# Stick-breaking attention in one inference step: two narrow tiles of each head run as one of 64 columns

## The chip, the core and the metric

The kernel runs on one core of a Trainium2 chip. A core has a matrix engine (PE, with its weight loads shown apart as PEld), a vector engine (DVE), an activation engine (ACT), a general engine (POOL) and a queue that issues most transfers (SP). The engines run side by side, each in its own program order, and wait for one another through semaphores. The metric is the device time of one execution in microseconds (us), as the median of several runs; lower is better.

## What is computed

One layer of a hybrid decoder: a combined input projection, stick-breaking attention in 8 heads of 128 beside gated linear attention in 4 heads, gates, and an output projection, for a prompt of 16 learned and 1024 given positions and for 32 sample positions with a paged cache. The change concerns only the prompt's attention:

```python
def stick_break_weights(z, mask):
    sp = jnp.where(mask, jax.nn.softplus(z), 0.0)
    later = lax.cumsum(sp, axis=z.ndim - 1, reverse=True) - sp
    return jnp.where(mask, jnp.exp(jax.nn.log_sigmoid(z) - later), 0.0)

def sb_attend(qb, qpos, k, v, kpos, bias):
    a = stick_break_weights(sb_logits(qb, k, bias), kpos[None, :] < qpos[:, None])
    return jnp.einsum('bhqk,bkhd->bqhd', a.astype(v.dtype), v)
```

A query sees only keys at strictly earlier positions. The weight of a key needs the sum of the softplus values of all later keys, so key tiles are worked from the last to the first, and a tile hands a running sum (the carry) to the one before it.

## The kernel before, in words

**The stage.** Eight heads follow one another. For each head the projections of v, k and q (`inproj`, L331 to L348) run as 24 steps each; a step, called a beat, is six wide matmuls (L342 to L344). Everything else of the stage is woven between the beats: generators are put on a list with `W.spawn`, and `W.beat()` runs those that are due. A `yield n` in a generator means "go on n beats later". The tile framework then fixes one order for each engine; an engine waits at the head of its queue, and nothing behind overtakes.

**The tiles.** A head's 1024 prompt queries are two halves, qi 1 (positions 528 to 1039) and qi 0 (positions 16 to 527). Keys lie in nine tiles of 126 keys (`KT`) in 128 rows; row 0 of a tile carries the running sum and row 127 is empty. `attend` (L631) spawns a tile for each pair (qi, j) in `ORDER` (L641): (1,8) down to (1,0), then (0,4) down to (0,0), with 2 to 5 beats between spawns by width. Because of the causal mask the first tile of each half is a sliver: (1,8) has 32 query columns and (0,4) has 24. Then come 158 and 150 columns, 284 and 276, 410 and 402, and 512.

**A tile** (`attend_tile`, L578): three matmuls make the logits z (L589 to L591; all products here are split into a high and a low part). DVE and ACT form softplus (L595 to L598), POOL clears what the mask excludes (L601). Two beats later ACT copies the carry out of the previous tile's z into row 0 (L607), waiting beat by beat until it is there; `split_tmp` makes the high part on ACT (L574) and the low part on DVE (L575). `D1` = 4 beats later two matmuls with the triangle `ntri0` add the sums to z (L610, L611); ACT takes the exponential (L615), POOL masks again (L617), and it is split again. `D2` = 6 beats later three matmuls with the values V add the tile's part into the output bank O (L623 to L625). O is one bank with one buffer; the first tile of a half takes it, and after tile j = 0 ACT copies it out (L628) and SP stores it (L629).

**Around it.** `head` (L663) makes the k tiles from the projection (`split_k`, L685, eight casts on ACT and eight subtractions on DVE for a head) and has k and v stored (`tok_out`); `load_v` (L554) reads v back by key tile, into V (L566, L568). `sample_q` (L648) copies q and a small product `zns` of the samples out. On DVE, the logits of the samples against the cached pages (`z_feed`, L464, the tile `jk`) are spread over this stage and the next at one page each two beats.

Of the kernel before, what the change touches and what calls it, by code (L numbers as in the profile page):

```python
# [10 lines left out]
F32 = mybir.dt.float32  # L11
# [5 lines left out]
ALU = mybir.AluOpType  # L17
# [3 lines left out]
P = 128  # L21
# [6 lines left out]
NSMP = NB * NT  # L28
T = META + SEQ + NSMP
REAL = META + SEQ  # L30
# [10 lines left out]
KT = 126  # L41
# [43 lines left out]
def hybrid_step(ctx: ExitStack, tc: tile.TileContext, x_prompt, x_sample, cache_k, cache_v, state_gla,  # L85
# [3 lines left out]
    nc = tc.nc  # L89
    mm = nc.tensor.matmul  # L90
    vec, act, pool = nc.vector, nc.scalar, nc.gpsimd
# [17 lines left out]
    W = Weaver()  # L109

    def stage(nm, dt=F32):
        return stg.tile([P, 384], dt, tag="stg", name=nm)
# [39 lines left out]
    znd = dram.tile([NSMP, HEADS, NSMP], F32, name="znd")  # L152
# [37 lines left out]
    with tc.tile_pool(name="xp", bufs=2) as xp, tc.tile_pool(name="xps", bufs=5, space=PSUM) as xps:  # L190
# [336 lines left out]
    with tc.tile_pool(name="sp", bufs=1) as sp, tc.tile_pool(name="sps", bufs=1, space=PSUM) as sps:  # L527
# [26 lines left out]
        def load_v(h, V, behind):  # L554

            for c in range(3):
                st = stage(f"vr{h}_{c}")
                sv = st[:].rearrange("p (a d) -> p a d", d=P)
                nt = 3 if c < 2 else 2
                src = new_v_prompt[0, 0, :, h, :]  # L560
                pool.memset(st[:], 0.0)
                nc.sync.dma_start(sv[1:KT + 1, :nt], src[c * 378:c * 378 + nt * KT].rearrange("(a p) d -> p a d", p=KT))
                if c == 2:
                    nc.sync.dma_start(sv[1:33, 2, :], src[8 * KT:REAL])
                vs = slice(3 * c, 3 * c + 3)
                ins = act.copy(V[0][:, vs, :], sv)  # L566
                tc.add_manual_dep(ins.ins, behind.name, NOSYNC, reason="behind")
                vec.tensor_tensor(V[1][:, vs, :], sv, V[0][:, vs, :].bitcast(F32), ALU.subtract)  # L568
                yield 1

        def split_tmp(X, rows, n, nm):
            a = sp.tile([P, 512], F32R, tag="hi", bufs=3, name=f"hi_{nm}")
            b = sp.tile([P, 512], F32R, tag="lo", bufs=3, name=f"lo_{nm}")
            act.copy(a[:rows, :n], X)  # L574
            vec.tensor_tensor(b[:rows, :n], X, a[:rows, :n].bitcast(F32), ALU.subtract)  # L575
            return a, b

        def attend_tile(h, qi, qlo, qhi, j, jmax, q, kt, V, carry, O):  # L578
            nm = f"{h}_{qi}_{j}"
            k0 = j * KT  # L580
            nk = P
            c0 = max(qlo, k0)
            col = c0 - qlo
            n = qhi - c0
            qs = slice(c0 - META, c0 - META + n)
            ks = slice(j * P, j * P + nk)
            z = sps.tile([P, 512], F32, tag="z", bufs=4, name=f"z{nm}")
            zz = z[:nk, :n]
            mm(zz, kt[0][:, ks], q[0][:, qs], start=True, stop=False)  # L589
            mm(zz, kt[0][:, ks], q[1][:, qs], start=False, stop=False)  # L590
            mm(zz, kt[1][:, ks], q[0][:, qs], start=False, stop=True)  # L591
            bias = bias0[:nk, h:h + 1]
            xt = sp.tile([P, 512], F32, tag="X", bufs=3, name=f"X{nm}")
            X = xt[:nk, :n]
            vec.tensor_scalar(X, zz, bias, 30.0, ALU.add, ALU.min)  # L595
            act.activation(X, X, AF.Exp)
            act.activation(X, X, AF.Ln, bias=1.0)
            vec.scalar_tensor_tensor(X, zz, bias, X, ALU.add, ALU.max)  # L598
            w = min(n, k0 + KT - c0)
            if w > 0:  # L600
                pool.affine_select(X[:, :w], X[:, :w], [[1, w]], ALU.is_gt, 0.0, base=c0 - k0 + 1, channel_multiplier=-1)  # L601
            yield 2
            if j < jmax:
                while carry.get(qi, (None,))[0] != j + 1:
                    yield 1
                _, cz, ccol = carry[qi]
                act.activation(X[0:1, ccol - col:], cz[0:1, :], AF.Copy, scale=-1.0)  # L607
            sh, sl = split_tmp(X, nk, n, "s" + nm)
            yield D1
            mm(zz, ntri0[:nk, :nk], sh[:nk, :n], start=False, stop=False, skip_group_check=True)  # L610
            mm(zz, ntri0[:nk, :nk], sl[:nk, :n], start=False, stop=True, skip_group_check=True)  # L611
            carry[qi] = (j, zz, col)
            yt = sp.tile([P, 512], F32, tag="X", bufs=3, name=f"Y{nm}")
            Y = yt[:nk, :n]
            act.activation(Y, zz, AF.Exp, bias=bias)  # L615
            if w > 0:
                pool.affine_select(Y[:, :w], Y[:, :w], [[1, w]], ALU.is_gt, 0.0, base=c0 - k0 + 1, channel_multiplier=-1)  # L617
            ah, al = split_tmp(Y, nk, n, "a" + nm)
            yield D2
            if j == jmax:  # L620
                O[qi] = sps.tile([P, 512], F32, tag="O", name=f"O{h}_{qi}")
            o = O[qi]
            mm(o[:, col:], V[0][:nk, j, :], ah[:nk, :n], start=(j == jmax), stop=False, skip_group_check=True)  # L623
            mm(o[:, col:], V[0][:nk, j, :], al[:nk, :n], start=False, stop=False, skip_group_check=True)
            mm(o[:, col:], V[1][:nk, j, :], ah[:nk, :n], start=False, stop=(j == 0), skip_group_check=True)  # L625
            if j == 0:
                st = sp.tile([P, 512], F32, tag="X", bufs=3, name=f"ost{h}_{qi}")
                act.copy(st[:], o[:])  # L628
                nc.sync.dma_start(od[h][:, qlo - META:qhi - META], st[:])  # L629

        def attend(h, q, kt, V):  # L631

            carry, O = {}, {}
            for qi, j in ORDER:
                qlo, qhi = ((16, 528), (528, REAL))[qi]
                n = qhi - max(qlo, j * KT)
                W.spawn(attend_tile(h, qi, qlo, qhi, j, (qhi - 1) // KT, q, kt, V, carry, O))
                yield 2 if n < 100 else 3 if n < 200 else 4 if n < 450 else 5

        D1, D2 = 4, 6  # L640
        ORDER = [(1, j) for j in range(8, -1, -1)] + [(0, j) for j in range(4, -1, -1)]  # L641

        def values(h, behind):
            V = [sp.tile([P, 9, P], F32R, tag=f"V{i}", name=f"V{i}_{h}") for i in range(2)]
            W.spawn(load_v(h, V, behind))
            return V

        def sample_q(h, qsm, ks):  # L648

            ps = sps.tile([P, 512], F32, tag="z", bufs=4, name=f"qst{h}")  # L650
            nc.tensor.transpose(ps[:NSMP, 0:P], qsm[:], ident[:])
            qtok = stage(f"qtok{h}")[:NSMP, :P]
            act.copy(qtok, ps[:NSMP, 0:P])
            nc.sync.dma_start(qsd[:, h * P:(h + 1) * P], qtok)
            ps = sps.tile([P, 512], F32, tag="z", bufs=4, name=f"zn{h}")
            mm(ps[:NSMP, :NSMP], ks[:], qsm[:], start=True, stop=True)
            zns = sp.tile([NSMP, NSMP], F32, tag="zns", name=f"zns{h}")
            act.copy(zns[:], ps[:NSMP, :NSMP])
            nc.sync.dma_start(znd[:, h, :], zns[:])
            yield 4  # L660
            heads_ready.append(h)

        def head(h):  # L663
# [15 lines left out]
            kt = [sp.tile([P, KW], F32R, tag=f"k{i}", name=f"k{i}_{h}") for i in range(2)]  # L679
# [3 lines left out]
            ks = sp.tile([P, NSMP], F32, tag="ks", name=f"ks{h}")  # L683

            def split_k(raw, c, lo, hi):  # L685
                at, end = lo, min(hi, REAL)
                while at < end:
                    j, off = divmod(at, KT)
                    n = max(1, (end - at) // KT) if off == 0 else 1
                    w = min(KT - off, end - at)  # L690
                    d = [t[:, j * P:(j + n) * P].rearrange("p (a x) -> p a x", a=n)[:, :, off + 1:off + 1 + w] for t in kt]
                    r = raw[:, at - lo:at - lo + n * w].rearrange("p (a x) -> p a x", a=n)
                    act.copy(d[0], r)
                    vec.tensor_tensor(d[1], r, d[0].bitcast(F32), ALU.subtract)
                    at += n * w
                if c == 2:
                    act.copy(ks[:], raw[:, REAL - lo:hi - lo])
                return
                yield
# [21 lines left out]
            V = values(h, copied[-1])  # L721
# [15 lines left out]
    with tc.tile_pool(name="gp", bufs=1) as gp, tc.tile_pool(name="gps", bufs=1, space=PSUM) as gps:  # L737
# [323 lines left out]
        for g in range(GH):  # L1061
            kt = gp.tile([P, T], F32, tag="k", name=f"gk{g}")
# [227 lines left out]
    with ExitStack() as out:  # L1290
# [347 lines left out]
        kept = []  # L1638
# [53 lines left out]
```

## Time and profile before

| | |
|---|---|
| median of 3 runs | 2067.45 us (2066.13 to 2067.91) |
| the profiled execution | 2066.38 us, its span 2064.6 us |
| matmuls (PE) in the program | 12507, busy 2024.8 us |
| heads, start of tile (1,8) to start of the next head's | 92.0 to 94.3 us |
| the tiles (1,8) and (0,4) | 8 matmuls each in each of 8 heads |

The span starts with the first instruction of the program and ends with the last; 1.8 us of the execution's time lie around it. The attention stage reaches from 116 us to about 860 us. A row of the timeline gives the start and the duration of an instruction or of a run of like ones; the end of a matmul is modelled, so the distance from one start to the next tells more than the duration.

### The profile page before, as it was taken

What the parts mean: (1) busy time and instruction counts of PE and PEld (TensorE: products, weight loads), DVE (VectorE), ACT (ScalarE), POOL (GpSimd) and SP (SyncE); (2) the same over time, 40 slices, a digit from 0 to 9 for tenths busy, and PEclk for the clock granted to TensorE, in tenths of its full rate; (3) what the DMA queues carried; (4) which work ended last, traced back from release to release, by engine and by line L of the source; (5) the groups of instructions that cost most, each with busy time, mean ns of one, the idle gap of its engine ahead of it and who ended that gap; (6) DMA issues with size and microseconds to landing.
All of it is one profiled execution on the core that took longest, in us unless ns stands there. A gap on an engine that the chain in (4) does not pass through costs nothing.

```text
span 2064.6 us, 41985 instructions
## 1 busy us (share of the span) xinstructions
PE 2024.8 (98%) x12507; PEld 1863.6 (90%) x12507; DVE 1552.7 (75%) x6282; ACT 953.4 (46%) x2293; POOL 84.6 (4%) x304
## 2 busy tenths in 40 slices
PE   6999999999999999999999999999999999999998
PEld 5999999999999998999999999998888898788776
DVE  7368989888988989899798897978544347454576
ACT  7355555565655656433534335343433325332332
POOL 0012000101000000000000000000000000000000
PEclk9999999999999999999999999999999999999999
DMA  6354454544455442533433433335776666452485
GB/s 202 103 139 148 139 159 133 171 132 147 146 160 146 140 124 76 139 102 82 108 100 79 125 82 110 98 82 155 236 233 231 220 222 200 139 166 74 129 271 202
DMA packets 371821, 301.85 MB, mean 146 GB/s; under 512 B 42360, under 2 KB 312104, under 8 KB 371592
## 3 DMA queue, kind: packets, MB, share of 16 engines
q1 hardware_dynamic: 371288, 298.64, 48.6%
q8 instruction: 98, 1.61, 0.3%
q14 instruction: 131, 1.07, 0.2%
q10 hardware_dynamic: 304, 0.53, 0.1%
HBM read 241.75 MB, written 57.31 MB: 145 GB/s over the span
## 4 chain that ended last, share of the span: by engine, by line
PE 75%; DVE 12%; DMA 6%; ACT 3%; issue 3%; SPq 0%; POOL 0%; DVEq 0%; ACTq 0%; POOLq 0%
PE acc_g L342 5%; PE acc_g L343 5%; PE acc_g L344 5%; DVE jk L464 5%; PE b L1593 4%; PE b L1595 4%; PE b L1594 4%; PE acc_k L342 3%; PE acc_k L344 3%; PE acc_k L343 3%; PE acc_v L342 2%; PE acc_q L342 2%; PE acc_q L344 2%; PE acc_q L343 2%; PE acc_v L344 2%
## 5 line engine op out<-in xcount | busy, mean ns | idle before, releaser
L464 DVE SCALAR_TENSOR_TENSOR jk<-kp,qb 128x128 f32<-128x128 f32 x2048 | 593.8, 290 | 43.5 <-DMA qb<-qsd 1.7
L342 PE MATMUL acc_g<-hT,wh_g 128*128 128x368 f32 (+2 forms) x768 | 251.4, 327 | 0.5 <-DVE ga L389 0.5
L343 PE MATMUL acc_g<-hT,wh_g 128*128 128x368 f32 (+2 forms) x768 | 247.6, 322 | 0.0
L344 PE MATMUL acc_g<-hT,wl_g 128*128 128x368 f32 (+2 forms) x768 | 247.1, 322 | 0.0
L1593 PE MATMUL b<-ring,f 128*128 128x512 f32 x416 | 164.3, 395 | 3.5 <-ACT gx L521 1.4
L464 DVE DVE_READ_ACCUMULATOR jk<-kp,qb 128x1 f32 x2048 | 167.6, 82 | 0.0
L1594 PE MATMUL b<-ring,f 128*128 128x512 f32 x416 | 162.6, 391 | 0.0
L1595 PE MATMUL b<-ring,f 128*128 128x512 f32 x416 | 162.1, 390 | 0.0
L342 PEld LDWEIGHTS acc_g<-hT,wh_g 128*128 128x128 f32 x768 | 144.5, 188 | 13.3 <-issue 10.8
L343 PEld LDWEIGHTS acc_g<-hT,wh_g 128*128 128x128 f32 x768 | 144.6, 188 | 1.1 <-issue 0.4
L1395 DVE TENSOR_TENSOR ring<-wr,ring 128x512 fp32r<-128x512 f32 x104 | 71.3, 689 | 98.4 <-ACT ring L1394 97.7
L344 PEld LDWEIGHTS acc_g<-hT,wl_g 128*128 128x128 f32 x768 | 144.5, 188 | 0.0
L342 PE MATMUL acc_gv<-hT,wh_gv 128*128 128x400 f32 (+2 forms) x384 | 130.5, 340 | 0.0
L1394 ACT CAST ring<-wr 128x512 fp32r<-128x512 f32 x104 | 64.1, 620 | 139.3 <-PE b L1595 77.0
L342 PE MATMUL acc_k<-hT,wh_k 128*128 128x384 f32 (+1 forms) x384 | 126.4, 329 | 0.0
L343 PE MATMUL acc_gv<-hT,wh_gv 128*128 128x400 f32 (+2 forms) x384 | 125.3, 326 | 0.0
L342 PE MATMUL acc_q<-hT,wh_q 128*128 128x368 f32 (+2 forms) x384 | 125.1, 326 | 0.0
L344 PE MATMUL acc_gv<-hT,wl_gv 128*128 128x400 f32 (+2 forms) x384 | 124.8, 325 | 0.0
L344 PE MATMUL acc_k<-hT,wl_k 128*128 128x384 f32 (+1 forms) x384 | 124.7, 325 | 0.0
L343 PE MATMUL acc_k<-hT,wh_k 128*128 128x384 f32 (+1 forms) x384 | 124.5, 324 | 0.0
L344 PE MATMUL acc_q<-hT,wl_q 128*128 128x368 f32 (+2 forms) x384 | 123.4, 321 | 0.0
L343 PE MATMUL acc_q<-hT,wh_q 128*128 128x368 f32 (+2 forms) x384 | 123.4, 321 | 0.0
(454 smaller groups left out, 5294.3 us busy)
## 6 DMA issues: line engine op xcount, KB each, us to landing
kp<-in_cache_k_dram SPq DMA_DIRECT2D x512, 64.0 KB
vr<-in_cache_v_dram SPq DMA_DIRECT2D x64, 512.0 KB
tf<-in_w_out_dram SPq DMA_DIRECT2D x64, 256.0 KB
td<-tf SPq DMA_DIRECT2D x64, 256.0 KB
qb<-qsd SPq DMA_DIRECT2D x64, 256.0 KB
wr_g<-in_w_in_dram SPq DMA_DIRECT2D x64, 256.0 KB
wr<-td SPq DMA_DIRECT2D x56, 256.0 KB
wr<-in_w_out_dram SPq DMA_DIRECT2D x48, 256.0 KB
```

The costliest lines, as they stand in the source:

```text
L342: mm(acc[c][:, :n], wh, hh[k][:, lo:hi], start=(k == 0), stop=False)
L343: mm(acc[c][:, :n], wh, hl[k][:, lo:hi], start=False, stop=False)
L344: W.mark = mm(acc[c][:, :n], wl, hh[k][:, lo:hi], start=False, stop=(k == NK - 1)).ins
L464: ins = vec.scalar_tensor_tensor(jk[:], kp[:], 1.0, qbs[h, b][:, t, :], ALU.mult, ALU.mult, accum_out=zt[:, t, NPG - 1 - i:NPG - i])
L1394: act.copy(wh, r)
L1395: vec.tensor_tensor(wl, r, wh.bitcast(F32), ALU.subtract)
L1593: mm(bk[:], ah, wh, start=first and k == 0, stop=False, skip_group_check=True)
L1594: mm(bk[:], ah, wl, start=False, stop=False, skip_group_check=True)
L1595: mm(bk[:], al, wh, start=False, stop=last and k == 7, skip_group_check=True)
```

## The change

The two slivers of a head become one tile of 64 columns, run as (1,8). Its columns 0 to 31 are the last 32 queries of half 0 and its columns 32 to 63 the last 32 queries of half 1. In its key tile, rows 1 to 31 hold keys 1008 to 1038 as before, and rows 32 to 55 hold copies of the 24 keys of tile 4 that half 0 needs, put there by two copies on POOL (L727 of the change) and, for V, by one more DMA in `load_v` (L565). The mask is one select over 64 columns and one clearing of 32 rows by 32 columns (`causal`). The query columns are read in two runs of 32 (`queries`).

After the triangle, ACT copies half 0's carry out at once into a small tile `cy` (L630), which takes the buffer of `ks`; half 1's carry is read from z as before. The output of the 64 columns goes to the output bank O, and ACT copies it out into `ob` (L648); then tile (1,7) takes the bank for half 1, and later (0,3) for half 0. When a half is done, DVE adds its 32 columns of `ob` into the staged output (L657), and the store follows. `ORDER` loses (0,4). The copy `zns` of the samples moves from a buffer of its own into the shared staging buffers.

```diff
             if c == 2:
-                nc.sync.dma_start(sv[1:33, 2, :], src[8 * KT:REAL])
+                nc.sync.dma_start(sv[1:32, 2, :], src[8 * KT:REAL - 1])
+                nc.sync.dma_start(sv[32:56, 2, :], src[4 * KT:4 * KT + 24])
...
+            both = j == 8
             c0 = max(qlo, k0)
             col = c0 - qlo
-            n = qhi - c0
+            n = 64 if both else qhi - c0
...
+            def queries(t):
+                if both:
+                    return t[:].rearrange("p (a x) -> p a x", a=2)[:, :, 480:512]
+                return t[:, qs]
+
+            def causal(t):
+                if both:
+                    t = t.rearrange("p (a x) -> p a x", a=2)
+                    pool.affine_select(t, t, [[1 - 24, 2], [1, 32]], ALU.is_gt, 0.0, base=24, channel_multiplier=-1)
+                    pool.memset(t[0:32, 0, :], 0.0)
+                elif w > 0:
+                    pool.affine_select(t[:, :w], t[:, :w], [[1, w]], ALU.is_gt, 0.0, base=c0 - k0 + 1,
+                                       channel_multiplier=-1)
...
-            carry[qi] = (j, zz, col)
+            if both:
+                kept = sp.tile([P, NSMP], F32, tag="ks", name=f"cy{h}")
+                act.copy(kept[0:1, :], z[0:1, 0:32])
+                carry[0], carry[1] = (4, kept, 480), (8, z[:, 32:64], 480)
+            else:
+                carry[qi] = (j, zz, col)
...
+            if both:
+                o = sps.tile([P, 512], F32, tag="O", name=f"Ob{h}")[:, :n]
+                mm(o, V[0][:, j, :], ah[:, :n], start=True, stop=False, skip_group_check=True)
+                mm(o, V[0][:, j, :], al[:, :n], start=False, stop=False, skip_group_check=True)
+                mm(o, V[1][:, j, :], ah[:, :n], start=False, stop=True, skip_group_check=True)
+                O[2] = sp.tile([P, 64], F32, tag="ob", name=f"ob{h}")
+                act.copy(O[2][:], o)
+                return
...
                 act.copy(st[:], o[:])
+                vec.tensor_tensor(st[:, 480:512], st[:, 480:512], O[2][:, 32 * qi:32 * qi + 32], ALU.add)
                 nc.sync.dma_start(od[h][:, qlo - META:qhi - META], st[:])
...
-        ORDER = [(1, j) for j in range(8, -1, -1)] + [(0, j) for j in range(4, -1, -1)]
+        ORDER = [(1, j) for j in range(8, -1, -1)] + [(0, j) for j in range(3, -1, -1)]
...
-            zns = sp.tile([NSMP, NSMP], F32, tag="zns", name=f"zns{h}")
-            act.copy(zns[:], ps[:NSMP, :NSMP])
+            zns = stage(f"zns{h}")[:NSMP, :NSMP]
+            act.copy(zns, ps[:NSMP, :NSMP])
...
                 if c == 2:
+                    for t in kt:
+                        pool.tensor_copy(t[:, 8 * P + 32:8 * P + 56], t[:, 4 * P + 1:4 * P + 25].bitcast(F32))
                     act.copy(ks[:], raw[:, REAL - lo:hi - lo])
```

The orders below are those of the built programs, without times. A row gives the source line (of its own program, so L610 before is L626 in the change), the operation, the tile written and the tiles read, and the shape.

The first place is PE in the first head, at the end of half 1 and the start of half 0; `z_0_4` is the logit bank of tile (0,4), `O_0` the output bank of half 0. Before:

```order
L589 MATMUL z_0_4_2278<-q_0_1072,k_0_842 128x24
L590 MATMUL z_0_4_2278<-q_0_1073,k_0_842 128x24
L591 MATMUL z_0_4_2278<-q_0_1072,k_0_843 128x24
...
L610 MATMUL z_0_4_2278<-hi_s_0_4_2332,ntri_825 128x24
L611 MATMUL z_0_4_2278<-lo_s_0_4_2333,ntri_825 128x24
...
L623 MATMUL O_0_2617<-hi_a_0_4_2444,V_0_1306 128x24
L624 MATMUL O_0_2617<-lo_a_0_4_2445,V_0_1306 128x24
L625 MATMUL O_0_2617<-hi_a_0_4_2444,V_0_1307 128x24
```

In the change the same places hold the next tile, (0,3):

```order
L605 MATMUL z_0_3_2288<-q_0_1074,k_0_842 128x150
L606 MATMUL z_0_3_2288<-q_0_1075,k_0_842 128x150
L607 MATMUL z_0_3_2288<-q_0_1074,k_0_843 128x150
...
L626 MATMUL z_0_3_2288<-hi_s_0_3_2343,ntri_825 128x150
L627 MATMUL z_0_3_2288<-lo_s_0_3_2344,ntri_825 128x150
...
L651 MATMUL O_0_2631<-hi_a_0_3_2445,V_0_1308 128x150
L652 MATMUL O_0_2631<-lo_a_0_3_2446,V_0_1308 128x150
L653 MATMUL O_0_2631<-hi_a_0_3_2445,V_0_1309 128x150
```

The eight matmuls of (0,4) are gone, and all of half 0 moves up by one tile; the projection's matmuls around them stand as before.

The second place is PE in the first head where the 64 columns leave the output bank and tile (1,7) takes it. In the change:

```order
L644 MATMUL Ob_1643<-hi_a_1_8_1443,V_0_1308 128x64
L645 MATMUL Ob_1643<-lo_a_1_8_1444,V_0_1308 128x64
L646 MATMUL Ob_1643<-hi_a_1_8_1443,V_0_1309 128x64
L342 MATMUL acc_v_2_1312<-hT_153,wh_v_2_1600 128x304
...
L651 MATMUL O_1_1739<-hi_a_1_7_1588,V_0_1308 128x158
L652 MATMUL O_1_1739<-lo_a_1_7_1589,V_0_1308 128x158
L653 MATMUL O_1_1739<-hi_a_1_7_1588,V_0_1309 128x158
```

Both wrote one bank `O_1` before, without a copy between; now ACT's copy of `Ob` stands between them. There are 29 other matmuls between L646 and L651.

The third place is ACT in the second head at the time when half 0 ends and the k tiles of the third head are cast (`k_2`; `st_k` are k's stores, `wh_q` the projection's weights). Before, the run of casts stands ahead of the exponential of (0,2) and the split of (0,1):

```order
L574 CAST hi_s_0_2_4335<-X_0_2_4180 128x276
L543 COPY st_k_0_4371<-tk_k_0_4370 128x384
L543 COPY st_k_1_4389<-tk_k_1_4388 128x384
L693 CAST k_2_3660<-kraw_0_4192 128x6
...
L693 CAST k_2_3660<-kraw_2_4259 128x32
L596 ACTIVATE X_0_0_4418<-X_0_0_4418 128x512
...
L615 ACTIVATE Y_0_2_4442<-z_0_2_4176,bias_827 128x276
L607 ACTIVATE X_0_1_4311<-z_0_2_4176 1x276
L574 CAST hi_a_0_2_4445<-Y_0_2_4442 128x276
L574 CAST hi_s_0_1_4451<-X_0_1_4311 128x402
```

In the change it stands behind them, ahead of the exponential of (0,1) and the split of (0,0):

```order
L575 CAST hi_s_0_1_4325<-X_0_1_4245 128x402
L722 CAST k_2_3656<-kraw_0_4179 128x3x126
...
L722 CAST k_2_3656<-kraw_2_4257 128x32
L543 COPY st_k_0_4371<-tk_k_0_4370 128x384
L612 ACTIVATE X_0_0_4358<-X_0_0_4358 128x512
...
L636 ACTIVATE Y_0_1_4432<-z_0_1_4241,bias_827 128x402
L623 ACTIVATE X_0_0_4358<-z_0_1_4241 1x402
L575 CAST hi_a_0_1_4435<-Y_0_1_4432 128x402
L575 CAST hi_s_0_0_4441<-X_0_0_4358 128x512
```

The same run of casts now meets the next tile of half 0, which is wider.

More of the change, by code (lines that the diff above doesn't have):

```diff
@@ L576, in split_tmp, with attend_tile @@
             return a, b
-        def attend_tile(h, qi, qlo, qhi, j, jmax, q, kt, V, carry, O):
+        def attend_tile(h, qi, qlo, qhi, j, q, kt, V, carry, O):
             nm = f"{h}_{qi}_{j}"
@@ L581, in attend_tile @@
             nk = P
+            both = j == 8
             c0 = max(qlo, k0)
             col = c0 - qlo
-            n = qhi - c0
+            n = 64 if both else qhi - c0
             qs = slice(c0 - META, c0 - META + n)
             ks = slice(j * P, j * P + nk)
+            def queries(t):
[10 more added lines that the diff above has]
+                                       channel_multiplier=-1)
             z = sps.tile([P, 512], F32, tag="z", bufs=4, name=f"z{nm}")
             zz = z[:nk, :n]
-            mm(zz, kt[0][:, ks], q[0][:, qs], start=True, stop=False)
-            mm(zz, kt[0][:, ks], q[1][:, qs], start=False, stop=False)
-            mm(zz, kt[1][:, ks], q[0][:, qs], start=False, stop=True)
+            mm(zz, kt[0][:, ks], queries(q[0]), start=True, stop=False)
+            mm(zz, kt[0][:, ks], queries(q[1]), start=False, stop=False)
+            mm(zz, kt[1][:, ks], queries(q[0]), start=False, stop=True)
             bias = bias0[:nk, h:h + 1]
@@ L599, in attend_tile @@
             w = min(n, k0 + KT - c0)
-            if w > 0:
-                pool.affine_select(X[:, :w], X[:, :w], [[1, w]], ALU.is_gt, 0.0, base=c0 - k0 + 1, channel_multiplier=-1)
+            causal(X)
             yield 2
-            if j < jmax:
+            jmax = (3, 7)[qi]
+            if not both:
                 while carry.get(qi, (None,))[0] != j + 1:
@@ L615, in attend_tile @@
             act.activation(Y, zz, AF.Exp, bias=bias)
-            if w > 0:
-                pool.affine_select(Y[:, :w], Y[:, :w], [[1, w]], ALU.is_gt, 0.0, base=c0 - k0 + 1, channel_multiplier=-1)
+            causal(Y)
             ah, al = split_tmp(Y, nk, n, "a" + nm)
@@ L636, in attend @@
                 n = qhi - max(qlo, j * KT)
-                W.spawn(attend_tile(h, qi, qlo, qhi, j, (qhi - 1) // KT, q, kt, V, carry, O))
+                W.spawn(attend_tile(h, qi, qlo, qhi, j, q, kt, V, carry, O))
                 yield 2 if n < 100 else 3 if n < 200 else 4 if n < 450 else 5
         D1, D2 = 4, 6
-        ORDER = [(1, j) for j in range(8, -1, -1)] + [(0, j) for j in range(4, -1, -1)]
+        ORDER = [(1, j) for j in range(8, -1, -1)] + [(0, j) for j in range(3, -1, -1)]
         def values(h, behind):
@@ L656, in sample_q @@
             mm(ps[:NSMP, :NSMP], ks[:], qsm[:], start=True, stop=True)
-            zns = sp.tile([NSMP, NSMP], F32, tag="zns", name=f"zns{h}")
-            act.copy(zns[:], ps[:NSMP, :NSMP])
-            nc.sync.dma_start(znd[:, h, :], zns[:])
+            zns = stage(f"zns{h}")[:NSMP, :NSMP]
+            act.copy(zns, ps[:NSMP, :NSMP])
+            nc.sync.dma_start(znd[:, h, :], zns)
             yield 4
```

## The prediction

> **What bounds the kernel now.** I read the page first: the busy times of the engines, then the chain of work that ended last, followed back from the last instruction, with its shares by engine.
>
> ```profile
> PE 2024.8 (98%) x12507; PEld 1863.6 (90%) x12507; DVE 1552.7 (75%) x6282; ACT 953.4 (46%) x2293; POOL 84.6 (4%) x304
> ...
> PE 75%; DVE 12%; DMA 6%; ACT 3%; issue 3%; SPq 0%; POOL 0%; DVEq 0%; ACTq 0%; POOLq 0%
> ```
>
> PE is busy for 98% of the span, but that is an average over several stages. The change touches only the attention stage, so I asked for the busy times by window: start:end, length, then busy time and count for PE, PEld, DVE, ACT and POOL, and at the end the granted clock.
>
> ```profile
> 116.00:393.00 277.00, 275.19 (x1685) 265.19 (x1684) 244.84 (x1104) 157.29 (x381) 32.34 (x106) 1.00 0.51 144
> ...
> 485.00:578.00 93.00, 91.91 (x562) 88.14 (x561) 82.45 (x378) 52.59 (x127) 7.84 (x27) 1.00 0.50 150
> ...
> 762.00:862.00 100.00, 99.34 (x609) 91.04 (x608) 90.32 (x418) 58.79 (x139) 8.40 (x35) 1.00 0.36 97
> ```
>
> PE is busy for 99% in each of them (275.19 of 277.00) at the full clock. DVE stands close behind: 244.84 of 277.00 is 88%, 90.32 of 100.00 is 90%. ACT has 43% of its time free (1 - 157.29/277.00), POOL far more. So a microsecond taken from PE here counts, as long as DVE, ACT and the carries still deliver in time. The waits of PE's weight loads in the whole stage (waiting line, releaser, total, times, longest) say how well they deliver now:
>
> ```profile
> PEld z L611 <- DVE lo_s L575: 6.2, 13, 1.1
> PEld z L610 <- ACT hi_s L574: 3.3, 5, 1.2
> PEld zn L656 <- issue: 2.2, 8, 0.3
> ```
>
> All eight heads together lose 6.2 + 3.3 = 9.5 us at the triangle matmuls. That is little against 750 us, but it says who is late when someone is: the split of the carried X, on ACT and DVE.
>
> **What the change removes.** The eight matmuls of tile (0,4) go in each of eight heads, 64 in all. A narrow matmul's duration in the timeline overlaps its neighbours', so I price it by starts. First the logits, with the projection's wide matmuls around them:
>
> ```profile
> 167.33 0.17 PE L589 MATMUL z<-q,k 128*128 128x24 f32 x1
> 167.36 0.26 PE L590 MATMUL z<-q,k 128*128 128x24 f32 x1
> 167.47 0.26 PE L591 MATMUL z<-q,k 128*128 128x24 f32 x1
> 167.58 0.42 PE L342 MATMUL acc_k<-hT,wh_k 128*128 128x384 f32 x1
> 167.84 0.34 PE L343 MATMUL acc_k<-hT,wh_k 128*128 128x384 f32 x1
> 168.02 0.33 PE L344 MATMUL acc_k<-hT,wl_k 128*128 128x384 f32 x1
> ```
>
> A wide matmul undisturbed takes 0.17 to 0.18 (167.84 to 168.02). From 167.33 to 167.84 stand three narrow ones and one wide one, 0.51; less 0.17 leaves 0.34 for three. It is not the 24 columns that cost: the first follows its neighbour almost free (0.03 to the next start), and the wide one behind starts its successor late (0.26 instead of 0.17). The triangle pair and the output triple, first start and second wide start behind:
>
> ```profile
> 175.35 0.17 PE L610 MATMUL z<-hi_s,ntri 128*128 128x24 f32 x1
> ...
> 175.75 0.33 PE L343 MATMUL acc_k<-hT,wh_k 128*128 128x384 f32 x1
> ...
> 831.63 0.17 PE L623 MATMUL O<-hi_a,V 128*128 128x24 f32 x1
> ...
> 832.13 0.33 PE L343 MATMUL acc_g<-hT,wh_g 128*128 128x368 f32 x1
> ```
>
> The pair: 0.40 - 0.17 = 0.23. The triple, here of the last head: 0.50 - 0.17 = 0.33. Together 0.34 + 0.23 + 0.33 = 0.90 us a tile, 0.112 us a matmul, and **8 x 0.90 = 7.2 us** for the stage.
>
> The Trainium skill has two rules that bear on this price, and they disagree. In "TensorE: Matmul & The Clock Gate", the section "Back-to-back issue gap" puts a matmul of up to 64 columns at an issue floor of about 25 ns, from which I estimate 64 x 0.025 = 1.6 us for the whole change. The section "LDWEIGHTS (loading the stationary operand)" of that page has a load take its columns over 1.2 in ns, so 107 ns for 128 columns, an estimate of 6.8 us. The trace's 0.112 us sides with the second.
>
> **What becomes wider.** The other sliver grows from 32 to 64 columns. A pair of 158 columns bounds it from above:
>
> ```profile
> 128.26 0.24 PE L610 MATMUL z<-hi_s,ntri 128*128 128x158 f32 x1
> ...
> 128.66 0.34 PE L343 MATMUL acc_v<-hT,wh_v 128*128 128x384 f32 x1
> ```
>
> 0.40 from start to start, as with 24 columns. So between 24 and 158 columns width costs PE nothing, and I take 0 for 64 (bounds 0 and 0).
>
> **What is added off PE.** These rows price it (busy, mean ns):
>
> ```profile
> L595 DVE TENSOR_SCALAR X<-z,bias 128x24 f32<-128x24 f32 x8 | 1.9, 239 | 0.0
> L575 DVE TENSOR_TENSOR lo_a<-Y,hi_a 128x32 fp32r<-128x32 f32 x8 | 1.7, 212 | 0.2
> L607 ACT ACTIVATE X<-z 1x32 f32<-1x32 f32 x8 | 1.4, 174 | 0.0
> L697 ACT COPY ks<-kraw 128x32 f32<-128x32 f32 x7 | 1.5, 218 | 0.2
> L628 ACT COPY ost<-O 128x512 f32<-128x512 f32 x16 | 9.4, 586 | 16.0 <-PE O L625 15.8 <-DVE lo_a L575 0.2
> L601 POOL TENSOR_SCALAR_AFFINE_SELECT X<-X 128x32 f32<-128x32 f32 x8 | 2.2, 280 | 117.5 <-DVE X L598 117.5
> ```
>
> - DVE: two additions of 128x32 a head, 2 x 0.21 = 0.42, against the four operations of (0,4), at up to 0.24 each, that go. DVE gets no fuller, but a head gets shorter by 0.90 too, so its share of 88 to 90% stays. The store now waits behind the addition; its buffer is one of the ring of three that X and Y use, and a head has two takings fewer from that ring than before. I take 0.
> - ACT: the carry copy, about 0.17, and the copy out of the bank, between 0.22 and 0.59 by the rows of 32 and 512 columns (near 0.22 at 64). The exponential, logarithm, casts and carry of (0,4) go, each about as long as the copies. The carry copy stands ahead of Y's exponential, and behind it waits the split of (1,7), some 0.2 us late; cover below.
> - POOL: two key copies of 24 columns, the rest widened, each nearest to 0.28; POOL is free for over 85% of the stage. The key copies wait for DVE's low parts of k, and the masks of X for (0,0) and of (0,1)'s Y stand queued behind them. This is a new wait on POOL, and the last rival is about it.
> - SP: one more transfer of 24 rows for V, behind other loads of V in the third and the seventh head. The `zns` copy takes a shared buffer; without cover it would lengthen the 2.2 us for all heads at `zn` above, which bounds it on the small side. I take 0 for both and price the transfer in a rival.
>
> The new wait I feared most is the output bank: (1,7) cannot take it before ACT has copied 64 columns out.
>
> ```profile
> 225.06 0.43 ACT L574 CAST hi_s<-X 128x284 fp32r<-128x284 f32 x1
> 225.07 0.26 PE L625 MATMUL O<-hi_a,V 128*128 128x32 f32 x1
> ...
> 229.96 0.23 PE L623 MATMUL O<-hi_a,V 128*128 128x158 f32 x1
> ```
>
> The sliver's output ends at 225.33; ACT is then in a cast until 225.49, and even a copy of 0.59 ends at 226.1. The bank is wanted at 229.96. Cover: 3.9 us. Were it gone, each head would stall for what is missing, with the projection's next beats queued behind L651 on PE.
>
> **The sum.** Profiled execution 2066.38 - 7.2 = 2059.2. The median of the runs stands 1.07 above that execution, so I forecast 2059.2 + 1.1 = **2060.3**. Its own range is 2058 to 2062.5: prices of 0.03 us a group (three groups, eight heads, 0.7 us) and the spread of the runs, with a little more upwards for the costs taken at 0.
>
> **The rivals.**
>
> *The stalls shrink too (chance 0.13).* Half 0's tiles start two beats earlier, and its chain of carries has one link of four beats less. The head's end, where the splits are late, gets more air. The second head's 1.66 us (shown below) stand at such a place, (0,1). If 4 of the 9.5 us go, somewhat under half, the time is 2060.3 - 4 = 2056.3. Against it: the waits name ACT and DVE, whose queues stay as full.
>
> *DVE and the transfers keep part (0.13).* In two of the windows the chain leaves PE for long stretches; these are its shares by line in 485:578 and 762:862, then one piece of it in the first, and rows of ACT and PE behind it:
>
> ```profile
> by line: DVE jk L464 11.1%; issue 8.4%; DMA qb<-qsd 6.4%; PE acc_k L342 6.0%; PE acc_k L344 6.0%; PE acc_k L343 6.0%; DMA vr<-out_dram 4.5%; PE acc_q L342 4.1%; PE acc_q L344 4.1%; PE acc_q L343 4.1%; DMA kp<-in_cache_k_dram 3.7%; DVE X L59
> ...
> by line: DVE jk L464 17.5%; issue 10.5%; PE acc_g L342 8.3%; PE acc_g L343 8.0%; PE acc_g L344 8.0%; DMA qb<-qsd 5.1%; DVE X L595 4.8%; DVE lo_s L575 4.6%; ACT X L596 2.8%; ACT X L597 2.8%; DVE wl_g L185 2.5%; ACT Y L615 2.1%; DVE X L598 2.
> ...
> 488.49 4.18 DMA vr<-out_dram
> 492.70 0.51 ACT L566 CAST V<-vr 128x384 fp32r<-128x384 f32 x1 [1.75 <-DMA vr<-out_dram]
> ...
> 505.63 0.40 PE L611 MATMUL z<-lo_s,ntri 128*128 128x284 f32 x1 [0.24 <-DVE lo_s L575]
> ...
> 510.57 0.45 PE L610 MATMUL z<-hi_s,ntri 128*128 128x410 f32 x1 [0.26 <-ACT hi_s L574]
> ```
>
> ACT waits 1.75 for V, and PE waits 0.24 and 0.26 a dozen microseconds later. If the added transfer does this to every head, 8 x 0.5 = 4.0 us go; if only half the heads, 2. With the two heads whose chain runs over DVE's `jk` giving nothing (2 x 0.9 = 1.8), it keeps about 4 of the 7.2: 2064.3. Against it: this wait, in the fifth head, is the only such one that I found, and DVE loses work in every head too.
>
> *The price is the first matmul's, not the group's (0.05).* By the step from 167.33 to 167.36 a narrow matmul costs 0.03 where its load hides behind a wide one. If the other five of a tile found such places too, 64 x 0.03 = 1.9, and 2065.5. Against it: the late wide matmul in all three groups. That the change removed fewer matmuls than it says would give the same; the order of the built program has them gone.
>
> *ACT's run of k casts makes the widest tile late, slower (0.05).* The casts for the next head stood ahead of the split of (0,1), and now stand ahead of that of (0,0), with POOL's key copies waiting for DVE in the same place. In the second head the run is now (ACT, then PE's loads for (0,1)):
>
> ```profile
> 187.10 0.60 ACT L693 CAST k<-kraw 128x114 fp32r<-128x114 f32 x3
> ...
> 191.29 0.42 ACT L574 CAST hi_a<-Y 128x276 fp32r<-128x276 f32 x1 [1.46 <-POOL Y L617]
> 191.62 0.52 ACT L574 CAST hi_s<-X 128x402 fp32r<-128x402 f32 x1
> ...
> 192.19 0.19 PEld L610 LDWEIGHTS z<-hi_s,ntri 128*128 128x128 f32 x1 [1.23 <-ACT hi_s L574]
> 192.81 0.19 PEld L611 LDWEIGHTS z<-lo_s,ntri 128*128 128x128 f32 x1 [0.43 <-DVE lo_s L575]
> ```
>
> Here a mask late on POOL made ACT wait 1.46 and the loads 1.23 + 0.43 = 1.66. If every head came to lose that, 8 x 1.66 = 13.3, and the time would be 2060.3 + 13.3 = 2073.6. It decides from 0.9 us a head (the gain gone) and is measurably slower from 1.4. Against it: 9.5 us over eight heads is 1.2 a head already counted in the time of before, and ACT has 43% of its time free to catch up.
>
> **How the numbers follow.** The forecast has 0.64, the rivals 0.13, 0.13, 0.05 and 0.05. A measurement of this kernel can tell about 0.2%, 4.1 us, from no change: faster means below 2063.3, slower above 2071.6. Faster: 0.64 + 0.13 = 0.77. Within: 0.13 + 0.05 = 0.18. Slower: 0.05. The range takes in the forecast, the shrunk stalls and the kept part, 0.90 of the chance less their outer tails: 2055.5 to 2065.
>
> **What would show it.** The profile should list 64 matmuls fewer, and from (1,8) to the next (1,8) a head about 0.9 us less than the 92.0 to 94.3 of before. Right about the cover: no load of L651 waiting for ACT's `ob`, no wait on `cy`. The first rival shows as fewer than 9.5 us of waits for hi_s and lo_s; the second as ACT waiting for `vr` in more heads; the last as waits at the triangle of (0,0), of 0.9 us or more a head. Wrong altogether would be a head that is shorter by 0.2 us with no new waits: then a narrow matmul is not worth 0.112.

## The result, and the profile after

| | before | after |
|---|---|---|
| median of 13 runs each | 2066.13 us (2062.32 to 2067.91) | 2071.12 us (2069.39 to 2073.27) |
| profiled execution, span | 2064.6 us | 2069.0 us |
| matmuls | 12507 | 12443 |

The change makes the kernel slower: ratio 1.0026, 95% interval 1.0018 to 1.0033. The 64 matmuls are gone, and the time went up by 5 us where 7.2 us less was forecast. The page of the changed kernel, busy times and then the chain's shares by engine:

```profile
PE 2023.6 (98%) x12443; PEld 1859.6 (90%) x12443; DVE 1550.6 (75%) x6266; ACT 947.9 (46%) x2269; POOL 89.1 (4%) x320
...
PE 72%; DVE 12%; DMA 7%; issue 4%; ACT 3%; SPq 1%; POOL 1%; DVEq 0%; POOLq 0%; ACTq 0%
```

The shares of busy time hardly move. PE's share of the chain falls from 75% to 72%, but that share is no measure of the time: two of the variants below, both faster than this kernel, have 72% (e7) and 66% (e8). What tells is the waits of PE's weight loads in the attention stage (waiting line, releaser, total, times, longest); L626 and L627 are the triangle's matmuls in the changed kernel:

```profile
PEld z L627 <- DVE lo_s L576: 8.9, 20, 0.9
PEld z L626 <- ACT hi_s L575: 8.0, 9, 2.5
PEld acc_v L342 <- ACT qsm L749: 2.4, 2, 2.1
```

The waits for the splits grew from 9.5 to 16.9 us, and a wait for `qsm` from 0.2 to 2.4. That is 7.4 + 2.2 = 9.6 us. By the timeline three places stand out.

**The end of the first head, (0,0).** The rows of POOL, ACT and PE, in this order:

```profile
190.82 0.88 POOL L401 TENSOR_SCALAR_AFFINE_SELECT lv<-lv 128x64 f32<-128x64 f32 x2
...
192.01 0.83 POOL L403 TENSOR_SCALAR_AFFINE_SELECT lv<-lv 128x64 f32<-128x64 f32 x2
192.81 0.29 POOL L601 TENSOR_SCALAR_AFFINE_SELECT Y<-Y 128x126 f32<-128x126 f32 x1
...
193.12 0.53 ACT L575 CAST hi_a<-Y 128x402 fp32r<-128x402 f32 x1 [2.00 <-POOL Y L601]
193.56 0.61 ACT L575 CAST hi_s<-X 128x512 fp32r<-128x512 f32 x1
...
194.22 0.49 PE L626 MATMUL z<-hi_s,ntri 128*128 128x512 f32 x1 [2.25 <-ACT hi_s L575]
195.26 0.79 PE L627 MATMUL z<-lo_s,ntri 128*128 128x512 f32 x1 [0.54 <-DVE lo_s L576]
...
196.17 0.52 PE L343 MATMUL acc_q<-hT,wh_q 128*128 128x384 f32 x1
196.49 0.52 PE L344 MATMUL acc_q<-hT,wl_q 128*128 128x384 f32 x1
```

POOL builds level masks (`lv`, from `level_masks`, for a later stage) ahead of the mask of (0,1). ACT waits 2.00 us for that mask with the split of (0,0) behind it, and PE stands for 2.25 and 0.54. Before, the same `lv` work delayed the narrower (0,1), and PE stood for 0.93 and 0.17 (the prediction's rows give the longer waits of its loads). And the price does not end with the stall: the wide matmuls behind it follow one another at 0.32 instead of 0.17. The busy times by window (PE, PEld, DVE, ACT, POOL, then the granted clock) show why:

```profile
194.00:196.00 2.00, 1.24 (x3) 0.83 (x4) 1.93 (x9) 0.17 (x1) 0.00 (x0) 0.76 0.07 15
196.00:198.00 2.00, 2.00 (x8) 2.00 (x7) 1.38 (x11) 1.30 (x2) 1.08 (x3) 0.50 0.58 197
198.00:200.00 2.00, 2.00 (x13) 2.00 (x13) 1.21 (x4) 0.62 (x1) 1.10 (x2) 0.89 0.60 94
```

The granted clock is at half for some 3 us. That loses 1.5 us: from the start of L627 to the next output matmul (L651) it takes 3.66 us here, and 2.20 in e3 below, where the same rows ran at full clock. With it the account closes: 9.6 + 1.5 = 11.1. The attention stage says the same. The first matmul of `acc_gk`, a projection of the next stage, starts 4.0 us later than before, where 7.2 earlier was forecast, so 11.2 are missing (before, then after):

```profile
870.52 0.34 PE L342 MATMUL acc_gk<-hT,wh_gk 128*128 128x400 f32 x1
```

```profile
874.53 0.34 PE L342 MATMUL acc_gk<-hT,wh_gk 128*128 128x400 f32 x1
```

Over the whole span it is 2069.0 - (2064.6 - 7.2) = 11.6 us.

**The triangle of (1,5), 410 columns.** ACT in the first head before (two rows), then ACT and PE after:

```profile
137.75 0.54 ACT L574 CAST hi_s<-X 128x410 fp32r<-128x410 f32 x1
138.19 0.62 ACT L182 CAST wh_k<-wr_k 128x512 fp32r<-128x512 f32 x1
```

```profile
137.82 0.60 ACT L182 CAST wh_k<-wr_k 128x512 fp32r<-128x512 f32 x1
138.33 0.53 ACT L575 CAST hi_s<-X 128x410 fp32r<-128x410 f32 x1
...
138.91 0.46 PE L626 MATMUL z<-hi_s,ntri 128*128 128x410 f32 x1 [0.85 <-ACT hi_s L575]
139.81 0.45 PE L627 MATMUL z<-lo_s,ntri 128*128 128x410 f32 x1 [0.44 <-DVE lo_s L576]
```

Two rows changed places: the cast of the next projection's weights now goes first, and the split that PE waits for is later by its length.

**The start of the third head.**

```profile
308.15 0.51 ACT L567 CAST V<-vr 128x384 fp32r<-128x384 f32 x1 [2.00 <-DMA vr<-out_dram]
308.57 0.19 ACT L749 ACTIVATE qsm<-acc_q 128x32 f32<-128x32 f32 x1
...
308.81 0.41 PE L342 MATMUL acc_v<-hT,wh_v 128*128 128x304 f32 x1 [1.95 <-ACT qsm L749]
```

A cast of V waits for its load with `qsm` queued behind it, and `qsm` holds a bank that PE's next projection needs. Before, `qsm` stood one row ahead of that cast.

### The profile page after: what moved, and what is told of

It reads as the page before. It is cut to its first block, busy times and chain, and to the rows that moved or that the text cites. A ratio compares the mean times of both kernels' runs of the same rounds, so it can differ in the third digit from the quotient of the medians.

```text
span 2069.0 us, 41791 instructions
## 1 busy us (share of the span) xinstructions
PE 2023.6 (98%) x12443; PEld 1859.6 (90%) x12443; DVE 1550.6 (75%) x6266; ACT 947.9 (46%) x2269; POOL 89.1 (4%) x320
## 4 chain that ended last, share of the span: by engine, by line
PE 72%; DVE 12%; DMA 7%; issue 4%; ACT 3%; SPq 1%; POOL 1%; DVEq 0%; POOLq 0%; ACTq 0%
PE acc_g L342 5%; PE acc_g L343 5%; PE acc_g L344 5%; DVE jk L464 5%; PE b L1624 4%; PE b L1626 4%; PE b L1625 4%; PE acc_k L342 3%; PE acc_k L343 3%; PE acc_k L344 3%; PE acc_v L342 2%; PE acc_v L343 2%; PE acc_v L344 2%; PE acc_gq L343 1%; PE acc_gq L342 1%
```

## The experiments

All were timed in five rounds against the kernel before; the ratios have 95% intervals. The theories first went by what was added: **A**, the addition on DVE; **B**, V's added transfer; **C**, POOL's key copies.

**e1, e2: the addition on DVE left out, and moved to POOL.** The reason for A was a new wait in the trace of the change, DVE's total for the addition:

```profile
DVE ost L657 <- ACT ost L656: 8.8, 6, 2.0
```

```diff
-                vec.tensor_tensor(st[:, 480:512], st[:, 480:512], O[2][:, 32 * qi:32 * qi + 32], ALU.add)
+                pool.tensor_tensor(st[:, 480:512], st[:, 480:512], O[2][:, 32 * qi:32 * qi + 32], ALU.add)
```

(e1 has only the first line of it.)

> The changed kernel without the two DVE additions of a head, so the output of the 64 columns is left out of the result; the order of all other work on PE, ACT and POOL stays but for a few rows. Theory A (the addition stands early in DVE's queue, waits there for ACT's copy of the output bank, 8.8 us in six waits, and DVE at 90% busy can't catch up, so the first tiles of the next head are late): the time falls by 4 to 8 us from 2071 to 2063 to 2067, and the waits of PE's loads for hi_s and lo_s fall from 16.9 us to about 10. Theory B (V is late through the added transfer) and theory C (POOL's key copies make masks late): no change, 2070 to 2072.

> The changed kernel with the two additions of a head on POOL instead of DVE; same result. Theory A: like e1, 2063 to 2067, unless POOL's masks queue behind the waiting addition, when some of it comes back. Theories B and C: no change, 2070 to 2072.

Measured: e1 2071.34 us, ratio 1.0025 (1.0015 to 1.0036); e2 2073.97, 1.0034 (1.0021 to 1.0046). A falls. In e1 DVE no longer waits there, and PE's waits are nearly the same:

```profile
PEld z L627 <- DVE lo_s L576: 8.1, 18, 0.8
PEld z L626 <- ACT hi_s L575: 7.8, 8, 2.4
```

DVE's 8.8 us of standing cost nothing that can be measured. On POOL (e2) the addition makes the kernel no faster either.

**e3: without the transfer of 24 rows of V.**

```diff
-                    nc.sync.dma_start(sv[32:56, 2, :], src[4 * KT:4 * KT + 24])
```

> The changed kernel without the added transfer of 24 rows of V, so the values of those 24 keys are left out. Theory B: ACT's waits for vr fall from 9.2 us to about 2 and the time by 2 to 4 us, to 2067 to 2069. Theories A and C: within 1 us of 2071, and ACT's waits for vr stay above 6 us, since V is late because SP's queue waits for DVE.

Measured 2071.32, ratio 1.0025 (1.0015 to 1.0035). B falls: the time stays. In its trace PE's wait for `qsm` is down to 0.6 us, but the waits for the splits are 18.1. ACT still waits for V nearly as long, in the trace of the change and in that of e3:

```profile
ACT V L567 <- DMA vr<-out_dram: 9.2, 6, 3.0
```

```profile
ACT V L566 <- DMA vr<-out_dram: 7.7, 6, 3.0
```

**e4: without POOL's key copies.**

```diff
-                    for t in kt:
-                        pool.tensor_copy(t[:, 8 * P + 32:8 * P + 56], t[:, 4 * P + 1:4 * P + 25].bitcast(F32))
```

> The changed kernel without POOL's two key copies of a head, so the logits of those 24 keys are left out (their key columns stay zero); all other orders stay as they are. Theory C: POOL's 19.1 us of waits for DVE's low parts of k go, masks come earlier, and the time falls by 2 to 4 us, to 2067 to 2069; the stall of 2.25 us at (0,0) of the second head goes. Theories A and B: within 1 us of 2071.

Measured 2073.17, ratio 1.0038 (1.0025 to 1.0051). C falls; PE still stood for 2.26 us at (0,0) of the first head (the expectation calls it the second). No addition taken alone is the cause. The next theories went by what was moved: **S**, the missing tile puts the queues in another order; **N**, the matmuls are worth 7.2 us and the additions together eat them; **P**, they are worth little; **Z**, the buffer that `zns` takes; **L**, the level masks.

**e5: the removal alone, in the kernel before.**

```diff
-        ORDER = [(1, j) for j in range(8, -1, -1)] + [(0, j) for j in range(4, -1, -1)]
+        ORDER = [(1, j) for j in range(8, -1, -1)] + [(0, j) for j in range(3, -1, -1)]
...
-                W.spawn(attend_tile(h, qi, qlo, qhi, j, (qhi - 1) // KT, q, kt, V, carry, O))
+                W.spawn(attend_tile(h, qi, qlo, qhi, j, 8 if qi else 3, q, kt, V, carry, O))
```

> The kernel before with tile (0,4) left out and nothing put in its place (24 columns of half 0 lose 24 keys and their carry), so 64 matmuls fewer and none of the additions. Theory S (the missing tile moves half 0 two beats ahead, the queues of ACT, DVE and POOL are put in another order, and the new order makes the splits late): 2066 to 2071, with longer waits for hi_s and lo_s than the 9.5 us of before. Theory N (narrow matmuls are worth 7.2 us, and what was added eats it): 2058 to 2061. Theory P (a narrow matmul is worth only 0.03 us): 2064 to 2066 with waits as before.

Measured 2067.92, ratio 1.0008 (0.9999 to 1.0017). Taking 64 matmuls out, and putting nothing in, gains nothing over the whole program. The waits of PE's loads (L610, L611 are the triangle here):

```profile
PEld z L611 <- DVE lo_s L575: 6.0, 13, 0.9
PEld z L610 <- ACT hi_s L574: 5.7, 7, 2.5
...
PEld acc_v L342 <- ACT qsm L718: 2.0, 2, 1.0
```

The stall of the first head's end is here too (its row stands in the last section), and the late `qsm`, and ACT waits for V:

```profile
ACT V L566 <- DMA vr<-out_dram: 7.7, 6, 3.8
```

So these come with the removal, not with the additions. Of the 7.2 us, the waits take 4.0 (11.7 + 2.0 against 9.5 + 0.2), and by the trace the stage does end 3.0 us earlier than before. S stands, but behind the stage the trace loses 4.2 us again. Of these, 0.9 is a wait for `gx` (ACT) and 1.5 a half clock at 1444 us, which e6's trace has too and the one of before has not; the rest stays open.

**e6: `zns` alone moved into the staging buffers, in the kernel before.**

```diff
-            zns = sp.tile([NSMP, NSMP], F32, tag="zns", name=f"zns{h}")
-            act.copy(zns[:], ps[:NSMP, :NSMP])
+            zns = stage(f"zns{h}")[:NSMP, :NSMP]
+            act.copy(zns, ps[:NSMP, :NSMP])
```

> The kernel before with zns alone moved into the shared staging buffers; no row of any queue moves. Theory Z (the buffer that zns takes makes the loads of V late, which ACT then waits for): ACT's waits for vr rise from 1.8 us toward 9 and the time by 2 to 4 us, to 2068 to 2070. Theories S and N: within 1 us of 2066.

Measured 2066.32, ratio 0.9999 (0.9990 to 1.0009). Z falls; this part costs nothing, as forecast.

**e7: the change with half 0 held back by two beats.**

```diff
                 yield 2 if n < 100 else 3 if n < 200 else 4 if n < 450 else 5
+                if (qi, j) == (1, 0):
+                    yield 2
```

> The changed kernel with half 0 held back by the two beats that (0,4) took, so that its tiles stand at the beats of before. Theory S: the k casts stand ahead of the split of (0,1) again, the waits fall toward 9.5 us, and the time to 2060 to 2065. Theories N and Z: within 1.5 us of 2071.

Measured 2064.24, ratio 0.9988 (0.9979 to 0.9997): 6.9 us less than the change, and a little faster than before. Two beats of standing back win what was lost. ACT at the end of the first head, before, after, and in e7:

```profile
202.13 0.62 ACT L182 CAST wh_v<-wr_v 128x512 fp32r<-128x512 f32 x1 [2.36 <-PE acc_q L343]
205.00 0.59 ACT L628 COPY ost<-O 128x512 f32<-128x512 f32 x1 [2.25 <-PE O L625]
```

```profile
204.23 0.59 ACT L656 COPY ost<-O 128x512 f32<-128x512 f32 x1 [4.63 <-PE O L653]
205.96 0.62 ACT L182 CAST wh_v<-wr_v 128x512 fp32r<-128x512 f32 x1 [1.14 <-PE acc_q L343]
```

```profile
200.47 0.62 ACT L182 CAST wh_v<-wr_v 128x512 fp32r<-128x512 f32 x1 [4.45 <-PE acc_q L343]
201.31 0.59 ACT L656 COPY ost<-O 128x512 f32<-128x512 f32 x1 [0.22 <-PE O L653]
```

In the change the copy of the output bank stands ahead of the weight cast and holds it back; in e7 the old order is there again. That this swap costs time is not shown: in the change, no matmul of PE waits for another engine from there until 236 us. What e7 wins is seen at the triangle, where the waits fall from 16.9 to 6.3 us. The waits for `qsm` do not fall (4.0 us), so they come with the missing tile, not with the two beats. The third and the seventh head give the price of a sliver: in neither trace does a matmul stand for another engine there (only PE's loads wait, once, 0.4 us before and 0.19 in e7). From the third head's start to the fourth's, before and in e7:

```profile
303.21 0.18 PE L589 MATMUL z<-q,k 128*128 128x32 f32 x1
...
395.24 0.18 PE L589 MATMUL z<-q,k 128*128 128x32 f32 x1
```

```profile
301.55 0.19 PE L605 MATMUL z<-q,k 128*128 128x64 f32 x1
...
392.52 0.19 PE L605 MATMUL z<-q,k 128*128 128x64 f32 x1
```

92.03 became 90.97, 1.06 us less; in the seventh it is 1.03.

**e8: the change with one level mask in each head, at its middle.**

```diff
-            yield 16
+            yield 72
...
-        W.spawn(level_masks(), 30, lasting=True)
+        W.spawn(level_masks(), 20, lasting=True)
```

> The changed kernel with POOL's level masks (lv) built one in each head, at the middle of the head, instead of one each 16 beats; the orders of PE and ACT stay as they are. Theory L (in the second head's preparation, at the end of the first head, the mask of (0,1) stands behind lv on POOL, the triangle of (0,0) stalls for 3.2 us, and PE then runs at half the granted clock for 2 us): the stall at (0,0) of the first head falls from 3.2 us to under 1, the clock stays at 1.00 behind it, and the time falls by 3 to 5 us, to 2066 to 2068. Other theories: within 1 us of 2071.

Measured 2068.15, ratio 1.0010 (1.0001 to 1.0019): 3.0 us less than the change. The mask of (0,1) now delays ACT by 0.38, and PE's triangle of (0,0) has only this left:

```profile
190.98 0.53 ACT L575 CAST hi_a<-Y 128x402 fp32r<-128x402 f32 x1 [0.38 <-POOL Y L601]
...
192.81 0.50 PE L627 MATMUL z<-lo_s,ntri 128*128 128x512 f32 x1 [0.22 <-DVE lo_s L576]
```

L stands, at the low end of what was expected: 2.8 us of stall and the half clock behind it. ACT's run of k casts is where it was, so that run is not what made this tile late.

**e9, e10, e11: the mends together, and the kernel before with two of them.** e9 is e7 with e8; e10 adds one edit, by which V's casts stand behind `qsm`:

```diff
-                    act.activation(qsm[:], ps[:, n:], AF.Copy, scale=QSCALE)
+                    copied.append(act.activation(qsm[:], ps[:, n:], AF.Copy, scale=QSCALE).ins)
```

> The changed kernel with both edits: half 0 held back by two beats (e7) and the level masks in the middle of the heads (e8). Theory S with L as two costs that add: 2064.2 - 3.0, so 2060.5 to 2062.5. If holding half 0 back already took the masks out of the way (L inside S): 2063 to 2065, as e7.

> As e9, and V's casts of a head stand behind the copy of qsm on ACT, which PE's next projection waits for. Theory Q (the 4.0 us of PE's waits for qsm in e7 come from V's late load at the head of ACT's queue): these waits fall under 1 us and the time by 2 to 4 us against e9, to 2058 to 2060. If V's load itself is what PE needs next: the waits move to another line and the time stays within 1 us of e9.

> The kernel before with the level masks in the middle of the heads and qsm ahead of V's casts, as a measure of what the two edits give without the change. Theory S: 1 to 2 us (the stall of 1.55 us at the end of the first head goes), 2064 to 2065.5; if the edits do as much here as behind the change, 2060 to 2062, and the change itself is worth nothing.

Measured: e9 2061.90, ratio 0.9982 (0.9973 to 0.9992); e10 2059.75, 0.9968 (0.9956 to 0.9980); e11 2064.93, 0.9992 (0.9983 to 1.0001). The times fell as expected, but that S and L are two costs that add is not shown. In e7's trace the first head's triangle of (0,0) has no stall left that e8's edit could take. The splits wait 6.3 us in e7 and 6.2 in e9. What differs is the sixth head's start, where PE waits 2.21 us for `qsm` in e7 and 1.03 in e9, and a half clock behind the longer wait (shown below). The intervals of e7 and e9 overlap. In e10 the waits for `qsm` are gone. The kernel before gets little from two of the edits: 1.2 us, not clear of noise.

**e12: the removal alone (e5), half 0 held at its old beats.**

> The kernel before with tile (0,4) left out as in e5 and half 0 held at its beats of before. Theory S with a price of 0.112 us for each of the 64 matmuls: 2059 to 2061. If removal alone is worth less, 2064 to 2066, and the price of a narrow matmul was wrong too.

Measured 2054.41, ratio 0.9940 (0.9927 to 0.9954), a larger gain than the theory expected. What is left of the waits:

```profile
PEld acc_v L342 <- ACT qsm L720: 1.7, 2, 1.3
PEld z L611 <- DVE lo_s L575: 1.6, 4, 0.6
...
PEld z L610 <- ACT hi_s L574: 0.2, 1, 0.2
```

The 9.5 us of before fell to 1.8, so the first rival, in which the stalls shrink too, is what removal does when half 0 keeps its beats: 7.2 + 7.7 - 1.5 (the longer wait for `qsm`) = 13.4, against 11.7 measured, and 12.2 at the end of the stage. Why the waits shrink below those of before is not shown. And e7, the same with the additions, is 9.8 us slower: the additions do cost, although taking one alone out of the shifted order gained nothing.

**e13, e14: the weight cast behind the split of (1,5).** In the built order of the change ACT casts the next k weights ahead of the split of (1,5) in five of the first seven heads. Before it was one of seven, and in e5 and e12 one too, so the additions do this. Four of them do not decide it alone: by the traces it is still five of seven with the addition on DVE, the transfer of V or the key copies left out (e1, e3, e4), and one of seven with `zns` alone moved (e6). The edit ties the cast (the second weight chunk after the split in the program) behind it:

```diff
-            act.copy(a[:rows, :n], X)
+            split_tmp.ins = act.copy(a[:rows, :n], X).ins
...
             sh, sl = split_tmp(X, nk, n, "s" + nm)
+            if (qi, j) == (1, 5):
+                hold.extend([split_tmp.ins, None])
...
-                tc.add_manual_dep(ins, hold.pop().name, NOSYNC, reason="behind")
+                first_in = hold.pop()
+                if first_in is not None:
+                    tc.add_manual_dep(ins, first_in.name, NOSYNC, reason="behind")
```

> The changed kernel with one order put back: ACT's cast of the next k weights (L182) stands behind the split of (1,5), 410 columns, in every head, as it did in six of the first seven heads before; PE's order is untouched. Theory W (the added work lets the scheduler put the weight cast, 0.6 us, ahead of the split in five of the first seven heads, and the triangle of (1,5) waits for it and for DVE's part): the 5.8 us of stalls at 410 columns fall under 2.5 and the time by 2 to 4 us, to 2067 to 2069. If the splits there are late for another reason: within 1 us of 2071.

> As e10, with the order of e13 as well. Theory W: the 4.1 us of stalls at 410 columns left in e10 fall to about 1, and the time from 2059.8 to 2056 to 2058, near the 2054.4 of e12. If not W: within 1 us of 2059.8.

Measured: e13 2069.53, ratio 1.0017 (1.0008 to 1.0026), 1.6 us less than the change, short of the 2 to 4 that were expected and with an interval that overlaps the change's. e14 2056.90, ratio 0.9955 (0.9942 to 0.9969), 2.9 us less than e10. In both the order is as meant, and PE's standing at the triangle of 410 columns falls by 1.4 us, from 3.7 to 2.3 in e13 and from 2.8 to 1.4 in e14, not to the small rest that theory W expected (its 5.8 and 4.1 us are waits of the loads). So the swap is a part of what makes these splits late; the rest stays open. e14 is the fastest version with the whole result of the change: 14.2 us below the change and 9.3 below the kernel before in its own comparison (8.0 below e11, the kernel before with two of the same edits). The waits of e14 (L630, L631 are its triangle):

```profile
PEld z L631 <- DVE lo_s L578: 3.4, 8, 0.7
...
PEld z L630 <- ACT hi_s L577: 1.3, 2, 0.9
```

## Why the prediction was wrong, point by point

- **The bound and the removal: not contradicted.** PE's matmuls went as counted. A head without such stalls became 1.03 to 1.06 us shorter in e7, up to 0.2 of it by shorter waits of the loads; the forecast was 0.90. The price of 0.03 falls: with the beats kept, removal gained 11.7 us. The table below sets the 7.2 us against the end of the stage.
- **The wider tile: right.** The triple of 64 columns and the wide matmul behind it take 0.52 from start to start:

```profile
116.21 0.19 PE L605 MATMUL z<-q,k 128*128 128x64 f32 x1
...
116.73 0.30 PE L343 MATMUL acc_v<-hT,wh_v 128*128 128x304 f32 x1
```

- **The sum, which takes 7.2 us off and adds nothing for waits: the step that failed.** It left the 9.5 us of waits at the triangle, and 0.2 for `qsm`, as they were, and took "what is added off PE" at 0. They became 16.9 and 2.4, with 1.5 for the half clock: 11.1 us. What was not priced is the order. In e5, which adds nothing, the waits grow by 4.0 us. The other 5.6 came with the additions, but with no single one: each was priced by its own time and wait, and taken one by one these gain nothing measurable (e1, e3, e4, e6). A queue that serves in order charges for a swap: the shown ones are POOL's `lv` ahead of a mask (e8) and a weight cast of ACT ahead of the split of (1,5) (e13, e14).
- **The argument "ACT has 43% of its time free": no cover.** Free time on average did not help the row that stood behind the wrong one.
- **The output bank: right.** No wait of PE for `ob` shows among the waits; the 0 for `zns` was right too (e6).
- **The first rival (stalls shrink)** came true only where half 0 kept its beats: 1.8 us of waits for the splits in e12, and 6.3 in e7, against 9.5.
- **The second rival (V)** had the right wait at the wrong cause: ACT's waits for `vr` did grow, from 1.8 to 9.2 us, but not through the added transfer (e3); with the removal alone they are 7.7 (e5). PE lost 2.2 us by it, in two heads.
- **The slower rival** had the place, the mask late on POOL ahead of the widest split, and the right sign of the result. The rows behind it, from 187 to 193 us, which the prediction places in the second head, are those of the first head's end. It was priced at 1.66 us in every head; it came as 2.8 us in one head, plus a half clock that the prediction did not know. What made the mask late was not the run of casts (e8 left it in place) nor the key copies (e4), but the level masks. That the result came near the rival's 2073.6 is therefore in part luck. The prediction showed the new order of ACT's rows and gave it no term in the sum.

The end of the stage by the traces (the first matmul of `acc_gk`, us), and what 7.2, the change of the waits for the splits and for `qsm`, and half clocks give:

| | starts at | against before | by the sum |
|---|---|---|---|
| before | 870.52 | | |
| the change | 874.53 | +4.0 | -7.2 + 7.4 + 2.2 + 1.5 = +3.9 |
| e5 | 867.50 | -3.0 | -7.2 + 2.2 + 1.8 = -3.2 |
| e7 | 866.35 | -4.2 | -7.2 - 3.2 + 3.8 + 1.5 = -5.1 |
| e12 | 858.36 | -12.2 | -7.2 - 7.7 + 1.5 = -13.4 |
| e14 | 858.66 | -11.9 | -7.2 - 4.8 - 0.2 = -12.2 |

So to 1.2 us the stage's end is the removal's 7.2 and the waits, and the waits are what the prediction lacked. In e7 a half clock stands behind the wait for `qsm` at the sixth head's start; up to the first wide matmul at full speed again it costs 1.5 us against the same rows of e9:

```profile
580.15 0.41 PE L342 MATMUL acc_v<-hT,wh_v 128*128 128x304 f32 x1 [2.21 <-ACT qsm L751]
...
582.00:584.00 2.00, 2.00 (x9) 1.42 (x8) 0.00 (x0) 0.43 (x3) 0.00 (x0) 0.50 0.30 87
```

What stays open: the time that e5 and e7 lose again behind the stage (e7's span is only 1.0 us shorter than that of before), and which of the additions together tip the order at (1,5).

## What to carry to other kernels

Where a scheduler fixes the order of in-order queues, taking work out is a change of order as well: compare the queues row by row before pricing the saving, above all what now stands ahead of the rows that the busiest engine waits for. To measure a removal by itself, leave its time slot empty (two beats here were worth 6.9 us in the change, and 13.5 without the additions). And a price list of the parts, each near zero, did not give the price of the whole here.

## What the hardware showed that was not expected

A stall can cost more than its length. After the 2.25 and 0.54 us in the first head the granted clock was 0.50 for the following matmuls, and one wait of 2.21 us was enough in e7. The same stall does not always do it: e1, e4 and e13 have the stall and the half clock, but in e2, e3 and e5 PE waited as long there, and the clock stayed. The rows are e5's:

```profile
192.99 0.49 PE L610 MATMUL z<-hi_s,ntri 128*128 128x512 f32 x1 [2.20 <-ACT hi_s L574]
...
194.00:196.00 2.00, 1.97 (x12) 1.93 (x13) 1.79 (x13) 1.01 (x2) 0.60 (x3) 1.00 0.52 172
```

The Trainium skill, "TensorE: Matmul & The Clock Gate", section "What's actually happening", describes such a gate: it halves the clock after an idle window of about 3.4 us, and the windows run free of the program. The chance in it agrees with the traces; the idle time does not, since here 2.25 us and 0.54 us with a matmul between, and 2.21 us alone, were enough.
